# A planner that charges TensorE for entering and leaving narrow tiles, in a two-layer diffusion step on one core

## The chip, the core and the metric

The kernel runs on one of the eight cores of one Trainium2 chip. The metric is the device time of one execution in microseconds (us). The core has four engines that compute: TensorE (PE in the profile; its weight loads are PEld), VectorE (DVE), ScalarE (ACT) and GpSimd (POOL). SyncE (SP) only issues DMAs here. Each engine runs its own list of instructions in order, and waits on semaphores where an operand comes from another engine or from a DMA.

## The reference

Two layers (DEPTH = 2) act on 640 tokens of width 2048, 128 of a prompt and 512 of a sample. Per layer, cut to what matters:

```python
shift, scale, gate = split(silu(c) @ w_ada[l] + b_ada[l], 3)      # adaLN
h = rmsnorm(x, norm_pre[l]) * (1 + scale) + shift
qa, ka, va, za, beta, alpha, cq, ckv, kpe, zb, xc, zc = split_cols(h @ w_in[l])
oa = delta_branch(...)    # 8 heads, gated DeltaNet, forward and backward
ob = mla_attend(...) * silu(zb)          # 4 heads of latent attention
oc = multiscale_pool(...) * silu(zc)     # 4 pooling groups
y = concatenate([oa, ob, oc]) @ w_out[l]
x = x + gate * rmsnorm(y, norm_post[l])

def gated_delta_chunked(...):            # inside delta_branch, per head and direction
    lmat = where(strict, einsum(kb, k) * decay, 0)
    sol = triangular_solve(lmat + eye, [kb * exp(gc), v * beta], lower, unit)
    s, o = scan over the chunks          # state update and output
```

The outputs are the two token streams after both layers, the normalised latents and rotary keys of the prompt, and the final states of its scans. Everything is float32.

## The kernel before

The kernel has no hand-written order. `Body` (line 502 on) calls operations through a recorder (`Sched.record`), in the order of the model: `consts`, `start`, then `phase_a(l)` and `phase_b(l)` for the two layers. `Sched.run` (line 350) then plans: it plays an event-driven model of the engines forward, and whenever an engine is free in that model it takes from the engine's heap the ready operation with the lowest priority number, which is the order of recording unless `later` shifts it. An operation becomes ready when its inputs are done in the model plus a latency from the table `LAT` (line 163: 0.45 us from TensorE to VectorE or ScalarE, 0.5 us back), and its buffers are granted. The length of an operation comes from `cost` (line 209): for TensorE a few hundredths of a us and the columns over 2400 per us, doubled for 3.4 us after an idle time of 3.4 us. The state of the port that VectorE and GpSimd share is the variable `port`. `issue` (line 469) emits the planned order, so all instructions of the trace carry line 499. The priorities, the latencies and the costs therefore decide what stands beside what, and nothing else does; the instructions that exist are the same whatever the costs, apart from operations that may go to one of two engines (`either`, line 309): copies and scalings to ScalarE or VectorE, and in `rest` (line 752) the remainder of a split to GpSimd or VectorE.

Full products are split in two float32r parts, high and low, so each costs three matmuls (`win_group`, line 783, for `w_in`; `product` in `phase_b` for `w_out`). In the trace they read from `slabr`, 128 rows by 256, 384 or 512 columns. These are the bulk of TensorE's work, about 12,000 of its 17,259 products and transposes. They depend on little, and the planner uses them to fill the time while TensorE waits for other things.

Narrow tiles are weights with fewer than 128 rows, or with 32 columns. They occur in three places:

- `ada_rows` (line 1457): the adaLN products, in bursts of 4 in `start` (256 columns wide) and of 16 later (128 wide), with a weight tile of 128x32 (`128*32` in the trace). After a burst `ada_sum` (line 1466) copies the sums out on ScalarE and transposes them.
- `delta` (line 1183), in each of the eight heads. The decay matrix of each of ten blocks of 128 tokens is inverted in steps. The 32x32 diagonal blocks go out to DRAM (`sd`, the name `d` in the trace), come back as 40 rows, and are solved on VectorE in 31 steps of two operations; the result goes to DRAM and comes back. Then TensorE joins the blocks: 20 products of 32x32, a VectorE copy of 128x160 (`T1`), 30 products of 32x32, copies on ScalarE and VectorE (`COPY slab<-psum 32x160` four times), 10 products of 64x64, a ScalarE copy (`T2`), and 10 more of 64x64. Between these bursts the planner puts full products of the next head's `head_in` (line 891), whose convolutions (`conv_tile`, line 841) are VectorE steps of 128x642.
- small transposes in `consts`, `start`, `consts2`, `gates` and `phase_b`.

After the joining, `delta` runs five dependent steps of the recurrence in both directions and ends in four and one transposes of the output.

Of the kernel before, what the change touches and what calls it, by code (L numbers as in the profile page):

```python
# [151 lines left out]
def cols(x):  # L152
    n = 1
    for s in x.shape[1:]:
        n *= s
    return n


class Sched:
# [190 lines left out]
    def run(self):  # L350
        self.prepare()
        ev = []
        seq = 0
        engs = ["PE", "DVE", "ACT", "POOL", "SP"]
        free = {e: True for e in engs}
        heap = {e: [] for e in engs}
        hw = 0.0
        bus = 0.0
        last, warm, port = -10.0, 0.0, 0.0

        def push(o):
            for e in {o.eng, *o.alts}:
                heapq.heappush(heap[self.ENG[e]], (o.pr, o))

        for op in self.ops:
            if op.need == 0:
                push(op)
        now = 0.0
        done = 0
        order = []  # L370
        again = []

        def retry(tags):
            for g in tags:
                for o in g.waiting.pop(g.next, ()):
                    o.parked = False
                    push(o)

        every = [g for g in self.tags.values() if g.space != "D"]
        while True:  # L380
            for e in engs:
                while free[e] and heap[e]:
                    pr, op = heapq.heappop(heap[e])
                    if op.placed or op.parked:
                        continue
                    new = [t for t in op.tiles if t.slot is None]
                    miss = None
                    for t in new:
                        if not self.grant(t):
                            miss = t  # L390
                            break
                        if t.tag.space != "D":
                            again.append(t.tag)
                    if miss is not None:
                        op.parked = True
                        miss.tag.waiting.setdefault(miss.n, []).append(op)
                        continue
                    op.placed = True
                    if self.ENG[op.eng] != e:
                        (op.eng, op.meth, op.a, op.k, op.cost, op.lock), = [(n, *x) for n, x in op.alts.items() if self.ENG[n] == e]  # L400
                    op.start = now
                    op.seq = len(order)
                    order.append(op)
                    if op.meth == "dma_start":
                        hw = max(hw, now) + 0.45
                        op.bus = max(bus, hw)
                        bus = op.bus + op.nbytes / 340e3
                        op.end = max(bus, hw + 0.3) + 2.0
                    else:
                        cost = op.cost  # L410
                        if e == "PE":
                            if now - last > 3.4:
                                warm = now + 3.4
                            if now < warm:
                                cost *= 2
                            last = now + cost
                        op.end = now + cost
                        if op.lock:
                            op.end = max(now, port) + cost
                            port = op.end  # L420
                    free[e] = False
                    heapq.heappush(ev, (now + op.cost if op.meth == "dma_start" else op.end, 0, seq, e))
                    heapq.heappush(ev, (op.end, 1, seq, op))
                    seq += 1
            if again:
                retry(again)
                again = []
                if any(free[e] and heap[e] for e in engs):
                    continue
            if not ev:  # L430
                break
            now = ev[0][0]
            rel = False
            while ev and ev[0][0] <= now + 1e-9:
                _, kind, _, x = heapq.heappop(ev)
                if kind == 0:
                    free[x] = True
                elif kind == 1:
                    done += 1
                    eng = self.ENG[x.eng]  # L440
                    for t in x.tiles:
                        t.left -= 1
                        if t.left == 0 and t.tag.space != "D":
                            heapq.heappush(ev, (now + self.FREE[t.tag.space], 3, seq, t))
                            seq += 1
                    for s in x.succ:
                        s.need -= 1
                        lat = self.LAT["DMA" if x.meth == "dma_start" else eng][self.ENG[s.eng]]
                        s.ready = max(s.ready, now + lat)
                        if s.need == 0:  # L450
                            heapq.heappush(ev, (s.ready, 2, seq, s))
                            seq += 1
                elif kind == 3:
                    g = x.tag
                    g.used[x.slot] = None
                    x.dead = True
                    while g.low < len(g.tiles) and g.tiles[g.low].dead:
                        g.low += 1
                    rel = True
                else:  # L460
                    push(x)
            if rel:
                retry(every)
        if done != len(self.ops):
            waits = [(o.i, o.eng, o.meth, [t.tag.name for t in o.tiles if t.slot is None]) for o in self.ops if not hasattr(o, "end") and o.need == 0]
            raise RuntimeError(f"stuck: {done} of {len(self.ops)}: {waits[:5]}")
        self.order = order
# [1199 lines left out]
```

## Time and profile before

| | before |
|---|---|
| median of 3 runs | 2635.76 us (2635.53 to 2638.45) |
| the profiled execution | 2642.71 us, its span 2640.6 us |
| mean granted clock of TensorE | 0.982 |
| TensorE busy | 2541.0 us (96%) |
| VectorE, ScalarE, GpSimd busy | 1664.4, 1026.8, 739.7 us (63%, 39%, 28%) |
| moved by DMA | 347.98 MB |

Span times run from the first instruction to the last of the profiled execution; the rest of its own time lies around them. A row such as `128*128 128x256` is a weight tile of 128 rows by 128 columns with a moving operand of 128x256; a float32 product is two records, a float32r product or a transpose is one. Starts overlap: a matmul's own duration includes its way through the array, so the pace is read from one start to the next.

### The profile page before, as it was taken

Reading aid. Unit: us, or ns where it says so; the run is one execution under the profiler, and the core shown is the slowest. Engines: PE = TensorE matmul, PEld = TensorE weight load, DVE = VectorE, ACT = ScalarE, POOL = GpSimd, SP = SyncE. Lnnn points to the kernel's source line nnn. Section 1 sums busy time; section 2 is a strip of 40 time slices with the busy share of each in tenths; the row PEclk is TensorE's granted clock in tenths of the full one; section 3 lists DMA queues with packets and bytes.
Section 4 is the critical chain, followed back from the end, with each engine's and each line's share of the span. In section 5 each row is a group of like instructions: output and inputs, shape, how many; then the busy total and the mean of one; then the engine's idle time right before and its main releaser. Section 6 shows DMA issues by size and latency. Waiting matters only on the chain.

```text
span 2640.6 us, 52982 instructions
## 1 busy us (share of the span) xinstructions
PE 2541.0 (96%) x20553; PEld 2380.4 (90%) x20553; DVE 1664.4 (63%) x4229; ACT 1026.8 (39%) x2789; POOL 739.7 (28%) x825
## 2 busy tenths in 40 slices
PE   4999999999999999999988999999999999999998
PEld 1689999999999998878888999999999999988888
DVE  3545556888888886332257365678878887755225
ACT  3233345444444432222247333444444444323222
POOL 0021112354333333220025211233444333334002
PEclk7999999999999999999998999999999999999999
DMA  9944444332343333896755434523433334336225
GB/s 314 335 108 110 133 116 121 96 95 83 92 103 101 102 91 100 235 271 173 190 182 157 126 95 126 149 78 91 101 103 90 91 92 103 84 84 194 92 75 191
DMA packets 541202, 347.98 MB, mean 132 GB/s; under 512 B 103826, under 2 KB 499734, under 8 KB 540310
## 3 DMA queue, kind: packets, MB, share of 16 engines
q1 hardware_dynamic: 540950, 344.59, 46.7%
q8 instruction: 162, 2.65, 0.4%
q14 instruction: 90, 0.74, 0.1%
HBM read 313.07 MB, written 31.46 MB: 130 GB/s over the span
## 4 chain that ended last, share of the span: by engine, by line
PE 80%; DMA 6%; DVE 3%; ACT 2%; POOL 1%; issue 1%; SPq 1%; DVEq 0%; ACTq 0%
PE psum L499 80%; DVE slab L499 3%; DMA slab<-d 2%; DMA slab<-in_w_in_dram 1%; DMA slab<-in_w_ada_dram 1%; ACT slab L499 1%; POOL slabr L499 1%; DMA slabW<-in_w_ada_dram 1%; DMA d<-slab 1%; SPq L499 1%; ACT slabr L499 1%; ACT slabW L499 0%; DMA slab<-in_x_sample_dram 0%; DVE slabV L499 0%; DMA slabW<-d 0%
## 5 line engine op out<-in xcount | busy, mean ns | idle before, releaser
L499 PE MATMUL psum<-slabr 128*128 128x384 f32 (+2 forms) x11760 | 2011.1, 324 | 2.3 <-DVE slabW L499 1.0
L499 PEld LDWEIGHTS psum<-slabr 128*128 128x128 f32 x11760 | 1778.2, 190 | 86.9 <-issue 23.5
L499 POOL TENSOR_TENSOR slabr<-slab,slabr 128x512 fp32r<-128x512 f32 (+3 forms) x428 | 482.8, 1136 | 1200.3 <-ACT slabr L499 878.8
L499 ACT ACTIVATE slabr<-slab 128x512 fp32r<-128x512 f32 (+3 forms) x731 | 393.3, 548 | 879.2 <-PE psum L499 726.5
L499 DVE TENSOR_TENSOR slabr<-slab,slabr 128x512 fp32r<-128x512 f32 (+3 forms) x404 | 262.8, 654 | 416.1 <-ACT slabr L499 363.8
L499 PE MATMUL psum<-slab 128*128 128x128 f32 (+4 forms) x4375 | 434.7, 256 | 56.7 <-DVE slab L499 31.9
L499 DVE TENSOR_TENSOR slab<-slab 128x5 f32<-128x5 f32 (+20 forms) x1298 | 473.2, 376 | 19.2 <-DMA slab<-d 3.9
L499 ACT ACTIVATE slab<-psum 128x128 f32<-128x128 f32 (+6 forms) x823 | 276.1, 351 | 492.5 <-PE psum L499 384.7
L499 PEld LDWEIGHTS psum<-slab 128*128 128x128 f32 (+4 forms) x4375 | 352.1, 140 | 97.5 <-DVE slab L499 39.3
L499 DVE SCALAR_TENSOR_TENSOR slab<-slab 128x5 f32<-128x5 f32 (+7 forms) x618 | 348.2, 572 | 42.9 <-ACT slab L499 33.9
L499 ACT ACTIVATE slab<-slab 128x642 f32<-128x642 f32 (+4 forms) x240 | 141.1, 603 | 62.3 <-DVE slab L499 55.7
L499 DVE COPY slab<-psum 32x160 f32<-32x160 f32 (+9 forms) x214 | 84.0, 399 | 112.7 <-PE psum L499 98.0
L499 DVE TENSOR_SCALAR slab<-slab 128x1 f32<-128x1 f32 (+7 forms) x363 | 111.4, 326 | 29.0 <-ACT slabW L499 16.2
L499 POOL TENSOR_SCALAR slab<-slabV,slab 128x128 f32<-128x128 f32 x128 | 58.1, 460 | 217.5 <-PE psum L499 216.9
L499 DVE SCALAR_TENSOR_TENSOR slab<-psum,slab 128x128 f32<-128x128 f32 (+1 forms) x216 | 80.1, 378 | 56.4 <-PE psum L499 54.5
L499 DVE TENSOR_REDUCE slab<-psum 128x4 f32<-128x16 f32 (+3 forms) x104 | 39.5, 380 | 106.5 <-PE psum L499 105.3
L499 PE MATMUL psum<-slab,slabW 32*32 32x32 f32 (+2 forms) x1216 | 80.8, 219 | 14.5 <-DMA slab<-d 7.8
L499 POOL TENSOR_TENSOR slab<-slab 128x640 f32<-128x640 f32 (+5 forms) x46 | 68.1, 1481 | 95.1 <-ACT slab L499 77.8
L499 ACT ACTIVATE slab<-psum,slab 128x256 f32<-128x256 f32 (+2 forms) x93 | 58.7, 641 | 78.3 <-DVE slab L499 74.6
L499 PEld LDWEIGHTS psum<-slab,slabW 32*32 32x32 f32 (+2 forms) x1216 | 66.3, 132 | 23.1 <-DMA slab<-d 10.7
L499 DVE SCALAR_TENSOR_TENSOR slab<-slab,psum 128x128 f32<-128x128 f32 (+2 forms) x160 | 62.0, 395 | 37.2 <-PE psum L499 25.9
L499 PE MATMUL psum<-slab,slabV 128*128 128x128 f32 (+1 forms) x352 | 72.4, 296 | 1.9 <-DVE slab L499 1.4
(61 smaller groups left out, 1384.5 us busy)
## 6 DMA issues: line engine op xcount, KB each, us to landing
slab<-in_w_in_dram SPq DMA_DIRECT2D x186, 512.0 KB
slab<-in_w_ada_dram SPq DMA_DIRECT2D x32, 1024.0 KB
slabW<-in_w_ada_dram SPq DMA_DIRECT2D x32, 1024.0 KB
slab<-in_w_out_dram SPq DMA_DIRECT2D x64, 512.0 KB
slabW<-d SPq DMA_DIRECT2D x64, 320.0 KB
slabV<-in_w_ada_dram SPq DMA_DIRECT2D x32, 512.0 KB
slabW<-in_w_ada_dram SPq DMA_DIRECT2D x32, 512.0 KB
d<-slab SPq DMA_DIRECT2D x32, 320.0 KB
```

The lines of the kernel that those rows point to most:

```text
L499: op.inst = getattr(getattr(nc, op.eng), op.meth)(*[real(x) for x in op.a], **{n: real(x) for n, x in op.k.items()})
```

## The change

The planner's loop gets one more state, `narrow`: whether TensorE's last placed operation had a narrow weight. Where the next one differs, its cost in the plan grows by 0.1 us on the way in and by 0.27 us on the way out. The instructions are as before but for the engine of those that may go to two.

```diff
@@ -356,7 +356,7 @@
-        last, warm, port = -10.0, 0.0, 0.0
+        last, warm, port, narrow = -10.0, 0.0, 0.0, False
@@ -409,6 +409,10 @@
                         cost = op.cost
                         if e == "PE":
+                            part = op.a[1].shape[0] < 128 or cols(op.a[1]) == 32
+                            if part != narrow:
+                                cost += 0.1 if part else 0.27
+                            narrow = part
                             if now - last > 3.4:
                                 warm = now + 3.4
```

The 17,259 products and transposes of TensorE stay, with 339 changes between narrow and other tiles before and 333 after. VectorE has 47 operations fewer and GpSimd 39 more; ScalarE has 8 more. Lines behind the change are four higher, so line 499 is 503 after.

The first place is VectorE in head 2 of layer 0, from the copy `T1` to the four copies that the 64x64 products need. `128x642` is a convolution step. Before:

```order
L499 COPY slab<-psum 128x160
L499 SCALAR_TENSOR_TENSOR slabV_3862<-psum,slab,slabW_3582 128x128 x2
L499 SCALAR_TENSOR_TENSOR slabW_3582<-psum,slab,slabW_3582 128x128 x2
L499 SCALAR_TENSOR_TENSOR slab<-slab 128x642
L499 STREAM_TRANSPOSE slabV_3862<-slabW_3582 32x160 x4
L499 SCALAR_TENSOR_TENSOR slab<-slab 128x642
L499 COPY slab<-psum 32x5x32 x4
L499 SCALAR_TENSOR_TENSOR slab<-slab 128x642
```

After, on the same stretch:

```order
L503 COPY slab<-psum 128x160
L503 SCALAR_TENSOR_TENSOR slabV_3862<-psum,slab,slabW_3555 128x128 x2
L503 SCALAR_TENSOR_TENSOR slabW_3555<-psum,slab,slabW_3555 128x128 x2
L503 SCALAR_TENSOR_TENSOR slab<-slab 128x642
L503 STREAM_TRANSPOSE slabV_3862<-slabW_3555 32x160 x4
L503 COPY slab<-psum 32x5x32 x4
L503 SCALAR_TENSOR_TENSOR slab<-slab 128x642
```

The convolution step that stood ahead of the four copies now stands behind them.

The second place is TensorE in head 5 of layer 0, from the first 32x32 burst to the first 64x64 burst, with full products (`slabr`) between. Before:

```order
L499 MATMUL psum<-slab,slabW_3582 32x32 x20
L499 MATMUL psum<-slabr 128x256 x3
L499 MATMUL psum<-slabr 128x384 x2
L499 MATMUL psum<-slabr 128x256 x6
L499 MATMUL psum<-slab 32x32 x30
L499 MATMUL psum<-slab 128x128 x4
L499 MATMUL psum<-slabr 128x256 x6
L499 MATMUL psum<-slabr 128x384 x5
L499 MATMUL psum<-slab,slabW_3582 64x64 x10
```

After:

```order
L503 MATMUL psum<-slab,slabW_3555 32x32 x20
L503 MATMUL psum<-slabr 128x256 x3
L503 MATMUL psum<-slabr 128x384 x4
L503 MATMUL psum<-slab 32x32 x30
L503 MATMUL psum<-slab 128x128 x4
L503 MATMUL psum<-slabr 128x384 x8
L503 MATMUL psum<-slab,slabW_3555 64x64 x10
```

Between the first two bursts 11 full products became 7, and between the second and third 11 became 8.

The third place is TensorE at the end of head 6 of layer 0, up to the four transposes of its output (the last row). Before:

```order
L499 MATMUL psum<-slabr 128x384 x2
L499 MATMUL psum<-slab 128x128 x4
L499 MATMUL psum<-slabr 128x384 x6
L499 MATMUL psum<-slabr 128x256 x12
L499 MATMUL psum<-slabr 128x384
L499 MATMUL psum<-slab 128x128
L499 MATMUL psum<-slabr 128x384 x7
L499 MATMUL psum<-slab,slabV_3862 128x128
L499 MATMUL psum<-slabr 128x384 x28
L499 MATMUL psum<-slab,slabV_3862 128x512
L499 MATMUL psum<-slab 128x128 x4
```

After:

```order
L503 MATMUL psum<-slabr 128x256 x2
L503 MATMUL psum<-slab 128x128 x4
L503 MATMUL psum<-slabr 128x256 x9
L503 MATMUL psum<-slabr 128x384 x10
L503 MATMUL psum<-slab 128x128
L503 MATMUL psum<-slabr 128x384 x2
L503 MATMUL psum<-slabr 128x256 x8
L503 MATMUL psum<-slab,slabV_3862 128x128
L503 MATMUL psum<-slabr 128x256 x4
L503 MATMUL psum<-slabr 128x384 x36
L503 MATMUL psum<-slab,slabV_3862 128x512
L503 MATMUL psum<-slab 128x128 x4
```

The full products in this stretch were 56 and are 71.

## Rows read from the trace of the kernel before

**Rows 1.** The page: span, engines (busy us, share, instructions), and chain by engine.
```profile
span 2640.6 us, 52982 instructions
...
PE 2541.0 (96%) x20553; PEld 2380.4 (90%) x20553; DVE 1664.4 (63%) x4229; ACT 1026.8 (39%) x2789; POOL 739.7 (28%) x825
...
PE 80%; DMA 6%; DVE 3%; ACT 2%; POOL 1%; issue 1%; SPq 1%; DVEq 0%; ACTq 0%
```

**Rows 2.** TensorE's waits: total us, times, longest us.
```profile
PE psum L499 <- DVE slab L499: 36.1, 20, 6.7
...
PE psum L499 <- DMA slab<-d: 7.8, 10, 1.4
```

**Rows 3.** Timeline, TensorE, change of layer: start, us, instruction [idle before, releaser].
```profile
1384.36 0.69 PE L499 MATMUL psum<-slab 128*128 128x128 f32 x2 [6.86 <-ACT slab L499]
```

**Rows 4.** Timeline, TensorE, an adaLN burst.
```profile
1058.55 0.60 PE L499 MATMUL psum<-slab 128*128 128x128 f32 x4
1059.08 1.08 PE L499 MATMUL psum<-slabW,slab 128*32 128x128 f32 x32
1060.09 0.71 PE L499 MATMUL psum<-slab,slabV 128*128 128x128 f32 x4
```

**Rows 5.** Timeline, TensorE, joining in head 2 of layer 0.
```profile
671.03 0.73 PE L499 MATMUL psum<-slab,slabW 32*32 32x32 f32 x40
671.69 1.93 PE L499 MATMUL psum<-slabr 128*128 128x256 f32 x14
673.55 2.17 PE L499 MATMUL psum<-slab 32*32 32x32 f32 x64
...
679.29 1.17 PE L499 MATMUL psum<-slab,slabW 64*64 64x64 f32 x20 [1.52 <-ACT slab L499]
```

**Rows 6.** Timeline, TensorE, joining in head 5 of layer 1.
```profile
2201.48 0.73 PE L499 MATMUL psum<-slab,slabW 32*32 32x32 f32 x40 [1.40 <-DMA slab<-d]
...
2204.34 3.52 PE L499 MATMUL psum<-slab 32*32 32x32 f32 x64
```

**Rows 7.** Windows: stretch, us, busy (instructions) of PE, PEld, DVE, ACT, POOL, clock, DMA.
```profile
132.00:138.00 6.00, 6.00 (x53) 4.07 (x51) 3.65 (x9) 1.20 (x2) 1.52 (x2) 1.00 0.13 30
2204.00:2211.00 7.00, 7.00 (x92) 6.46 (x92) 4.61 (x12) 3.20 (x9) 1.28 (x1) 0.59 0.17 26
```

**Rows 8.** Timeline, VectorE, the same stretch of head 2.
```profile
673.05 0.32 DVE L499 COPY slab<-psum 128x160 f32<-128x160 f32 x1
...
676.52 1.43 DVE L499 SCALAR_TENSOR_TENSOR slab<-slab 128x642 f32<-128x642 f32 x1
677.88 1.31 DVE L499 COPY slab<-psum 32x160 f32<-32x160 f32 x4
```

**Rows 9.** Timeline, TensorE, output transposes of head 6, layer 0.
```profile
1034.03 0.70 PE L499 MATMUL psum<-slab 128*128 128x128 f32 x4 [1.61 <-DVE slab L499]
```

**Rows 10.** Timeline, TensorE, adaLN products in `phase_b` of layer 0.
```profile
1094.07 1.08 PE L499 MATMUL psum<-slabW,slab 128*32 128x128 f32 x32 [1.49 <-DMA slabW<-in_w_ada_dram]
1095.08 5.52 PE L499 MATMUL psum<-slabr 128*128 128x384 f32 x34
1102.90 1.08 PE L499 MATMUL psum<-slabW,slab 128*32 128x128 f32 x32 [2.30 <-DMA slabW<-in_w_ada_dram]
```

**Rows 11.** Groups of TensorE by form: busy us, mean ns | idle before, releaser.
```profile
L499 PE MATMUL psum<-slabr 128*128 128x384 f32 x4800 | 1002.7, 344 | 1.0 <-ACT slabr L499 0.9
L499 PE MATMUL psum<-slabr 128*128 128x256 f32 x5520 | 799.5, 288 | 1.0 <-DVE slabW L499 1.0
```

**Rows 12.** Timeline, TensorE, the last adaLN products of the start.
```profile
138.15 0.64 PE L499 MATMUL psum<-slabW,slab 128*32 128x256 f32 x8
```

**Rows 13.** Timeline, VectorE and GpSimd, solve steps and a remainder.
```profile
654.43 0.23 DVE L499 TENSOR_TENSOR slab<-slab 40x87 f32<-40x87 f32 x1
...
654.85 1.08 DVE L499 TENSOR_TENSOR slab<-slab 40x87 f32<-40x87 f32 x1
...
654.54 1.29 POOL L499 TENSOR_TENSOR slabr<-slab,slabr 128x512 fp32r<-128x512 f32 x1 [2.04 <-ACT slabr L499]
```

## The prediction

> **What bounds the kernel.** I read the page's engine table and chain first. TensorE is busy for 2541.0 of 2640.6 us and carries 80% of the chain that ended last [rows 1]. So the time is TensorE's own work plus what it waits for, and an order can change only the second part, about 100 us. The table of waits says who ends them: VectorE in 20 of them (36.1 us) and the DMAs that bring back a head's solved blocks in 10 (7.8 us) [rows 2]. The timeline shows that a large share of the rest is structural: at the change of layer TensorE waits 6.86 us for the normalised rows [rows 3]. The new order has the same products, the same transposes and the same VectorE and ScalarE steps there, so that wait stays.
>
> **What the change does to the order.** No instruction is added or removed; the planner's clock for TensorE alone changes, by 0.1 us on entering and 0.27 us on leaving a narrow tile. It does not make the planner gather narrow tiles: the built orders have 339 changes between narrow and full tiles before and 333 after. What it does change is how much other work the planner believes has passed. The trace gives the true price. Four 128-wide products take 0.53 us up to a burst of 16 narrow ones (32 records), and that burst takes 1.01 us to the next start [rows 4]. The planner had this burst at 16 x (0.01 + 128/2400) = 1.01 us, and now has it at 1.38. So the old plan was right for this burst within the entry, while the new one is 0.37 us too long, or 0.28 us if the entry costs 0.09 us more than it was charged (0.53 against 4 x 0.109, the planner's price for the four transposes). For 20 products of 32x32 the old plan had 20 x 0.0668 = 1.34 us, the new one 1.71, and the trace has 0.66 us to the next start [rows 5]. The new clock overcharges bursts: where an answer is awaited across one, TensorE gets there 0.3 to 0.4 us earlier than planned; where a long chain on VectorE is awaited, the plan puts in other work.
>
> **Terms, on the profiled execution's 2642.7 us (span 2640.6 and 2.1 around it).** It lies 0.26% over the median of the runs, 2635.8; I take the same change off the median.
>
> Solve waits. A head's first 32x32 products wait for blocks that come back by DMA: 1.40 us in head 5 of layer 1 [rows 6], the longest of the ten. Between a head's last key-query product (line 1244) and this read, I counted TensorE's work at the paces of undisturbed neighbours: 72.6, 70.5 and 70.0 us in heads 3, 4 and 5 before, and 74.3, 71.3 and 75.5 us after, while VectorE's work in the same stretch is no longer than it was. The waits there are 0.97, 1.05 and 0.74 us in layer 0 and 0.78, 0.98 and 1.40 in layer 1 (the row, and five like it); the added 1.7, 0.8 and 5.5 us take off 5.5 of their 5.9 us. Bounds: 0 (VectorE late by as much) and 7.8, all such waits [rows 2].
>
> The clock behind a wait. After the 1.40 us wait the granted clock falls to 0.59 in the next stretch, the lower of the two levels (1.2 GHz) for most of it [rows 7]; the 64 small products take 3.52 us there [rows 6] against 2.17 in head 2 of layer 0, where no wait came before them [rows 5]. Their 1.35 us, and as much again for the full tiles about them, are 3 us that go with the wait. Bounds 0 and 3.
>
> VectorE in head 2. TensorE waits 1.52 us at the 64x64 products [rows 5] because VectorE does a 642-wide convolution step of 1.43 us just before the four copies (1.31 us) that these products need [rows 8]. The new order has that step behind the copies. The same happens in layer 1: 2 x 1.52 = -3.0 us. Bounds 0 and -3.0. In head 5 the new order puts such a step in front of other work that the copies follow; I charge the like of one head, 3.0 us over both layers, as the cost of queues that I cannot see. Bounds 0 and 8, twice the longest and a clock fall.
>
> End of the heads. The output of head 6 is awaited 1.61 us [rows 9] (1.27 us in layer 1). From its last product on, 56 fp32r products stood before its four transposes and 71 do now. At 5.52 us for 34 [rows 10] the 15 give 2.4 us, more than either wait: -2.9 us. The two waits for w_ada behind it, 1.49 and 2.30 us [rows 10], have 21 and 38 products before them in place of 14 and 34: 11 x 0.162 = -1.8 us. Bounds for both: 0 and -6.7.
>
> Prologue. Here the change costs. The planner's clock loses more to the many bursts of four, and 43 fewer full products stand before the last transposes of the start (144 stand behind them, 101 before); at 0.145 us, the busy time per 128x256 product [rows 11], that is 6.2 us of work put off. TensorE cannot win it all back by being early, since it waits for w_ada there. But the DMA engines are only 0.13 busy from 132 us on, so the last w_ada tile is there by then, and TensorE reads it at 138.15 [rows 7, 12]: it is 5 us behind its loads. So 5 of the 6.2 us are only moved, and +1.2 is lost. Bounds 0 and 6.2.
>
> Short trips. This is the term against the change. In each head's solve three answers are fetched across narrow bursts. Counted at 0.145 and 0.209 us (the busy time of a 128x384 product [rows 11]), the filler between the first two bursts falls from a mean of 1.73 to 1.31 us over the 16 heads, between the second and third from 2.31 to 1.99, and between the third and fourth from 1.76 to 1.30: 1.2 us a head, 19 us in all. In head 2 the copy ends at 673.37 us and TensorE reads it at 673.55 [rows 5, 8], so there is next to no spare there, and yet no wait is seen; the copy was late because VectorE was busy with a convolution step until it began at 673.05, while TensorE had sent its burst at 671.03 to 671.76. Elsewhere the answer takes 0.6 us less. I take a third, +6 us, because VectorE's waits are only 20 in the whole run. Bounds 0 and 19.
>
> Six fewer changes at 0.09 us: -0.5. The sum is -5.5 - 3.0 - 3.0 + 3.0 - 2.9 - 1.8 + 1.2 + 6.0 - 0.5 = -6.5 us: 2636.2 for the profile, 2629 for the median, 0.25% less. What a measurement of this kernel can tell from no change is about 0.2%, or 5.3 us.
>
> **A rule weighed.** The trace shows a change of tile size costing about 0.09 us on the way in [rows 4]. The Trainium skill, "TensorEngine Tiling (Array Packing)", section Key Properties, says that changing the tiling mode drains TensorE; it has no time for it. Were the drain as long as the planner's 0.37 us a pair, the new plan would be the true one, the short trips would lose nothing, and the sum by that reading would be -12.5 us; by the row it is -6.5.
>
> **Rivals.**
> No change that can be measured: the waits that go are given back elsewhere in the delta heads, half of the short trips' 19 us in place of a third and the prologue's 6.2 us in full; -6.5 + 3.5 + 5.0 = +2, about 2637. For it speaks that TensorE is full and the products are the same; against it that head 2 and the solve waits are placed differently in both layers.
> Slower, by short trips: TensorE comes to the three reads of each solve, and to the transposes behind each burst of adaLN products, before VectorE or ScalarE has answered. If two thirds of the 19 us become waits and four of these reach 1.4 us and pull the clock down at 3 us each, the sum is -6.5 + 6.5 + 12 = +12, 2648. It decides from the point where more than half of the trips have under 0.4 us to spare; the read at 673.55 speaks for it, the 20 waits against it.
> Slower, by the port: the new order has 39 more operations on GpSimd and 47 fewer on VectorE. A VectorE solve step of 0.23 us took 1.08 us while a GpSimd remainder of 1.29 us ran [rows 13], ending with it. If every added remainder held up a solve step by 0.85 us, the solves would grow by 39 x 0.85 = 33 us, 2 us in each head, less the 0.4 us that each remainder leaves on VectorE, 16 us: the solve waits come back and the sum is -6.5 + 8.5 + 6 = +8, 2644. The Trainium skill, "SBUF — State Buffer", section SBUF: two separate sides, says that the port pair that both share is locked for a whole instruction and the loser blocks; the trace agrees, at 1.08 against 0.23 us. Against it: the planner already holds the one engine for the other, and in heads 3 to 5 the VectorE work of the solve gets less.
>
> **Numbers.** Forecast (faster, -6 to -20) 0.44; no measurable change 0.34; slower by short trips 0.16; slower by the port 0.06. So faster 0.44, same 0.34, slower 0.22. The gains' far bounds are -7.8 - 3 - 3 - 6.7 = -20 with no cost, 2615; the cost side reaches 2648. The range is 2614 to 2648; the forecast's own is 2615 to 2630.
>
> **What would show it.** Right: waits for the solve's DMA under 3 us in all; no wait of 1.5 us at the 64x64 products of head 2; none over 0.5 us before head 6's transposes; the last start transposes near 142 us. Wrong: more than 30 waits for VectorE, or new stretches at the lower clock between 430 and 1030 us; the prologue ending with TensorE idle for more than 5 us beyond what it is; a solve step count as before with longer steps.

## The result and the profile after

The change makes the kernel slower: 2673.99 us median (2672.61 to 2674.70, 4 runs) against 2635.65 (2635.51 to 2638.45, 4 runs). The ratio is 1.0142, 95% interval 1.0125 to 1.016. The forecast was 2629 with a range to 2648, so the sign is wrong and the range misses the time by 26 us.

The profiled execution took 2672.61 us. Its page answers to [rows 1]:

```profile
span 2670.8 us, 52968 instructions
...
PE 2555.4 (96%) x20553; PEld 2389.0 (89%) x20553; DVE 1675.6 (63%) x4182; ACT 1024.9 (38%) x2797; POOL 788.5 (30%) x864
...
PE 79%; DMA 12%; DVE 5%; ACT 2%; SPq 1%; issue 1%; POOL 0%; DVEq 0%; ACTq 0%; POOLq 0%
```

The span is 30.2 us longer. TensorE does the same 20,553 records, yet is busy 14.4 us longer, so about half of the loss is hidden in "busy". In the chain the share of DMAs went from 6 to 12%. The table of TensorE's waits (total, times, longest) has more and other waits than [rows 2]:

```profile
PE psum L503 <- DVE slab L503: 33.8, 24, 6.0
PE psum L503 <- ACT slab L503: 14.4, 9, 6.8
PE psum L503 <- DMA slab<-d: 14.2, 12, 2.5
PE psum L503 <- DMA slabW<-in_w_ada_dram: 9.7, 16, 3.5
```

The waits for solved blocks rose from 7.8 to 14.2 us. Those for w_ada (this row and two smaller ones) rose from 13.6 to 17.5 us. Summed over the whole view, TensorE waits 100.2 us in place of 86.3.

Where it lies: I took the start of the same product in both traces at the borders of the stages. The heads of layer 0 (from the first transposes of head 0 to the last product of the first column group of `phase_b`) take 784.1 us in place of 765.2, those of layer 1 747.8 in place of 740.1, the start 1.5 us more, and the rest within 3 us. So 26.6 of the 30 us are in the heads. I split them by the pace of like pairs of neighbouring products at the full clock: 13.6 us are added waits, and 12.8 us are added time in stretches of low clock (26.1 us against 13.3). Everything else cancels. The trace's own records say nearly the same: in the heads the waits are 41.1 us against 27.9, and the granted clock is at its lower level for 51.2 us against 27.4, of which half is lost.

The stretches follow waits. This is TensorE in head 2 of layer 0, to be read against [rows 5]:

```profile
675.28 1.62 PE L503 MATMUL psum<-slabr 128*128 128x256 f32 x9
678.42 0.73 PE L503 MATMUL psum<-slab,slabW 32*32 32x32 f32 x40 [1.52 <-DMA slab<-d]
679.08 2.77 PE L503 MATMUL psum<-slabr 128*128 128x256 f32 x11
681.78 3.52 PE L503 MATMUL psum<-slab 32*32 32x32 f32 x64
684.95 2.59 PE L503 MATMUL psum<-slabr 128*128 128x256 f32 x10
687.47 2.03 PE L503 MATMUL psum<-slab,slabW 64*64 64x64 f32 x20
```

The 1.52 us wait that stood at the 64x64 products is gone, as forecast; but as much stands at the first 32x32 products now, where none was before, and the 64 records behind it (30 small products and four transposes) take 3.52 us instead of 2.17. The windows (stretch, us, five engines' busy time and instructions, granted clock, DMA share, GB/s) show the clock behind this wait, behind the wait for blocks in head 7, and behind a wait for w_ada:

```profile
679.00:694.00 15.00, 15.00 (x144) 13.71 (x138) 7.36 (x18) 4.63 (x12) 0.92 (x2) 0.54 0.38 102
1065.00:1076.00 11.00, 10.06 (x134) 9.17 (x135) 3.43 (x11) 1.22 (x3) 0.00 (x0) 0.53 0.21 54
1120.00:1127.00 7.00, 5.96 (x49) 5.61 (x50) 0.00 (x0) 0.00 (x0) 2.99 (x3) 0.51 1.06 267
```

That is the lower of the two levels (1.2 GHz) for nearly all of 15, 11 and 7 us. The waits ahead of the last two, on TensorE's timeline:

```profile
1065.93 1.10 PE L503 MATMUL psum<-slab,slabW 32*32 32x32 f32 x40 [2.54 <-DMA slab<-d]
...
1121.04 1.93 PE L503 MATMUL psum<-slabW,slab 128*32 128x128 f32 x32 [3.47 <-DMA slabW<-in_w_ada_dram]
```

The second answers to [rows 10], where the two waits were 1.49 and 2.30 us.

Why do the solved blocks come later? From the end of a head's solve on VectorE to the first 32x32 product it takes 11.5 us in the mean over the 16 heads, against 9.7 before. SyncE's queue shows one reason in head 7 of layer 0. Before:

```profile
1032.45 0.33 SPq L499 DMA_DIRECT2D slabV<-in_w_pool_dram  x1
1035.21 3.50 SPq L499 DMA_DIRECT2D d<-slab  x6
1039.07 4.74 SPq L499 DMA_DIRECT2D slab<-d  x9
```

After:

```profile
1052.30 0.33 SPq L503 DMA_DIRECT2D slabV<-in_w_pool_dram  x1
1052.72 2.11 SPq L503 DMA_DIRECT2D d<-slab  x5
1054.93 0.57 SPq L503 DMA_DIRECT2D slab<-in_w_in_dram  x1
1055.61 3.78 SPq L503 DMA_DIRECT2D slab<-d  x6
1059.50 0.99 SPq L503 DMA_DIRECT2D slab<-in_w_in_dram  x1
1061.65 2.32 SPq L503 DMA_DIRECT2D slab<-d  x3
```

The nine loads of the blocks went out in one piece before; now a w_in load stands among them and the last three leave 1061.65 to 1063.97 us, which is when the 2.54 us wait is made. The stores are late too: five of them leave from 1052.72 on, behind a w_pool load and behind the end of the solve at 1052.37, where all six left from 1035.21 on before, with the solve ending at 1037.60. In head 4 two w_in loads stand ahead of the stores:

```profile
823.30 7.76 SPq L503 DMA_DIRECT2D slab<-in_w_in_dram  x2
831.15 1.67 SPq L503 DMA_DIRECT2D d<-slab  x4
835.47 0.80 SPq L503 DMA_DIRECT2D slab<-d  x2
```

The second of them waits for its buffer until a GpSimd remainder is done. SyncE's waits in the stretch from 822 to 841 us say so:

```profile
SPq L503 <- POOL slabr L503: 9.1, 2, 6.9
```

The solve ended at 829.66 us and its first stores left at 831.15; before, the first left 1.75 us ahead of the end of the solve. Over the 16 heads, the last of the nine loads leaves SyncE 9.2 us after the end of the solve in the mean, against 7.4 before. That is the whole of the 1.8 us by which the mean trip grew.

### The profile page after: what moved, and what is told of

It reads as the page before. It is cut to its first block, busy times and chain, and to the rows that moved or that the text cites. A ratio compares the mean times of both kernels' runs of the same rounds, so it can differ in the third digit from the quotient of the medians.

```text
span 2670.8 us, 52968 instructions
## 1 busy us (share of the span) xinstructions
PE 2555.4 (96%) x20553; PEld 2389.0 (89%) x20553; DVE 1675.6 (63%) x4182; ACT 1024.9 (38%) x2797; POOL 788.5 (30%) x864
## 3 DMA queue, kind: packets, MB, share of 16 engines
q1 hardware_dynamic: 540950, 344.59, 46.1%
## 4 chain that ended last, share of the span: by engine, by line
PE 79%; DMA 12%; DVE 5%; ACT 2%; SPq 1%; issue 1%; POOL 0%; DVEq 0%; ACTq 0%; POOLq 0%
PE psum L503 79%; DVE slab L503 4%; DMA slabW<-in_w_ada_dram 3%; DMA slab<-d 2%; DMA slab<-in_w_in_dram 1%; SPq L503 1%; DMA slab<-in_w_ada_dram 1%; ACT slab L503 1%; DMA d<-slab 1%; DMA d<-slabV 1%; DMA slabW<-d 1%; DMA slabV<-in_w_ada_dram 1%; DMA slab<-in_x_prompt_dram 0%; POOL slabr L503 0%; DMA slab<-in_x_sample_dram 0%
## 5 line engine op out<-in xcount | busy, mean ns | idle before, releaser
L503 POOL TENSOR_TENSOR slabr<-slab,slabr 128x512 fp32r<-128x512 f32 (+2 forms) x469 | 532.5, 1145 | 1186.3 <-ACT slabr L503 898.7
L503 DVE TENSOR_TENSOR slabr<-slab,slabr 128x512 fp32r<-128x512 f32 (+3 forms) x363 | 250.3, 694 | 416.1 <-ACT slabr L503 386.3
L503 PE MATMUL psum<-slab 128*128 128x128 f32 (+4 forms) x4375 | 441.3, 257 | 61.9 <-DVE slab L503 30.5
L503 DVE TENSOR_TENSOR slab<-slab 40x240 f32<-40x240 f32 (+21 forms) x1298 | 482.1, 383 | 27.2 <-DMA slab<-d 11.5
L503 ACT ACTIVATE slab<-psum 128x128 f32<-128x128 f32 (+7 forms) x817 | 273.1, 350 | 511.1 <-PE psum L503 407.3
L503 DVE SCALAR_TENSOR_TENSOR slab<-slab 128x5 f32<-128x5 f32 (+7 forms) x618 | 350.7, 576 | 57.7 <-ACT slab L503 53.1
L503 DVE COPY slab<-psum 32x160 f32<-32x160 f32 (+7 forms) x220 | 88.1, 407 | 111.1 <-PE psum L503 99.1
L503 DVE TENSOR_SCALAR slab<-slab 128x1 f32<-128x1 f32 (+9 forms) x367 | 124.3, 358 | 23.1 <-ACT slabW L503 11.5
L503 POOL TENSOR_SCALAR slab<-slabV,slab 128x128 f32<-128x128 f32 x128 | 65.4, 519 | 241.4 <-PE psum L503 240.9
L503 PE MATMUL psum<-slab,slabW 32*32 32x32 f32 (+2 forms) x1216 | 82.5, 223 | 19.9 <-DMA slab<-d 14.2
L503 PEld LDWEIGHTS psum<-slab,slabW 32*32 32x32 f32 (+2 forms) x1216 | 68.3, 136 | 28.2 <-DMA slab<-d 17.4
```

What stands on the lines that cost most here:

```text
L503: op.inst = getattr(getattr(nc, op.eng), op.meth)(*[real(x) for x in op.a], **{n: real(x) for n, x in op.k.items()})
```

## The experiments

Each edit is against the changed kernel, unless it says otherwise. Ratios are to the kernel before, on the same chip. The first four ask which part of the charge costs, and whether its size matters.

**A tenth of the charge.**
```diff
-cost += 0.1 if part else 0.27
+cost += 0.01 if part else 0.027
```


> The charge is cut to a tenth: 0.01 us on the way in, 0.027 us on the way out. The plan's order still differs from that before from TensorE's operation 237 on. Theory A (size): the loss of 38 us comes from the planner's TensorE clock being 0.37 us too long for each burst, so a tenth of it costs a tenth at most: 2636 to 2640 us. Theory B (reshuffle): any small change of the clock reorders the eight delta heads of both layers, and which order comes out is luck; then this lies anywhere between about 2620 and 2675, and a value more than 6 us away from before with a charge this small speaks for B.

Measured: 2642.22 us, 1.0012 (0.9998 to 1.0026). That is 4 us over the kernel before on the same chip (2638.26), under the 6 us that were to speak for B, and 2 us over A's range. Size, then, by the bound set; but within it the waits for blocks are 13.3 us, nearly those of after.

**Only the narrow tiles of the heads.**
```diff
-part = op.a[1].shape[0] < 128 or cols(op.a[1]) == 32
+part = op.a[1].shape[0] < 128
```


> The full charge (0.1 and 0.27 us), but only for weights with fewer than 128 rows: the bursts of the delta heads and a few small transposes; the 32-column adaLN products are planned as before. In the trace of after the added time lies in the heads (20 us in layer 0, 10 in layer 1). Theory A (size, in the heads): as after, 2665 to 2680. Theory B (reshuffle): another order of the heads, so anywhere between 2620 and 2675.

Measured: 2662.38, 1.0087 (1.0066 to 1.0108): a little under what A said, and within B's wide bounds.

**Only the adaLN products.**
```diff
+part = op.a[1].shape[0] == 128 and cols(op.a[1]) == 32
```


> The full charge, but only for the 32-column adaLN products (128 rows); the bursts of the heads are planned as before. Theory A: the heads are not charged, so no more than the adaLN part of the loss is seen, 2633 to 2641. Theory B: the charge in the start alone shifts what is left over when the heads begin, so their order changes and the time can move by 6 us or more either way.

Measured: 2650.07, 1.0040 (1.0027 to 1.0053), over A's 2641, so B's reading fits better here. Yet the waits differ by place. Those for w_ada are 12.5 us with the charge in the heads alone and 16.2 with it on the adaLN products alone (13.6 before). Those inside the recurrence of the heads are 8.9 us in the first and 3.6 in the second (3.1 before, 7.7 after). For the recurrence this alone shows nothing of the charge: the plan without any charge and with the engine choice of before, further below, has 7.7 us there too.

**The charge, with the engine choice of the plan before.** Each operation that may go to one of two engines is fixed ahead of planning, from a list.
```diff
+for op, b in zip([o for o in self.ops if o.alts], side, strict=True):
+    if b == "1":
+        (op.eng, op.meth, op.a, op.k, op.cost, op.lock), = [(n, *x) for n, x in op.alts.items()]
+    op.alts = {}
```


> The full charge as in after, but each operation that may go to one of two engines goes where the plan before the change put it (245 operations differ between the two plans). Theory C (engine choice): the longer solves of heads 2, 3 and 5 (59.4, 59.5 and 60.9 us against 55.0, 56.8 and 55.7) come from VectorE steps held up by added GpSimd remainders, so at least half of the 38 us goes: 2655 or less, with solves within 1 us of before. Theory A: as after, 2665 to 2680. Theory B: anywhere between 2620 and 2675, with solves no shorter as a rule.

Measured: 2649.33, 1.0037 (1.0024 to 1.0050): most of the loss is gone, as C said. But not for C's reason: the solves of heads 2, 3 and 5 are 60.3, 49.5 and 56.9 us, one longer than in after and two shorter. It is the waits for blocks that went, to 5.9 us, and no low clock is left in the heads. The waits for w_ada are 23.0 us, more than in after, and those inside the recurrence 9.2.

The next two move only SyncE's queue; the order on the four computing engines is kept.

**w_in loads behind the solve's DMAs, on the plan of after and on that of before.**
```diff
+for sd in [t for t in self.tags["D"].tiles if t.shape == [3, 10, 128, 32]]:
+    trip = [o for o in order if sd in o.tiles][2:]
+    sp = [o for o in order if o.eng == "sync"]
+    i, j = sp.index(trip[0]), sp.index(trip[-1])
+    for w in sp[max(0, i - 3):j]:
+        if w.tiles[0].tag.name == "raw" and w not in trip:
+            ...   # move w behind trip[-1], but ahead of its first user
```


> The plan of after, with the instructions of TensorE, VectorE, ScalarE and GpSimd in exactly the order of after. Only SyncE's queue is changed: in each head the w_in loads that stand between or just ahead of the stores and loads of the solved blocks (34 loads over both layers) are moved behind them, as far as their first user allows. Theory Q (queue): in after a w_in load that waits for a GpSimd remainder stands ahead of the stores, so in head 4 they go out 1.5 us after the solve's end where they went out 1.75 us before it, and the blocks are read 10.2 to 13.6 us after the solve's end against 8.3 to 10.9 before; the queue then gives back most of the 6.3 us of added waits for solved blocks and the clock falls behind them: waits for blocks from 14.2 us to under 7, and 2650 to 2664. Theory S (solve length): the solves of heads 2, 3 and 5 are longer and that is what TensorE waits for; the return trip is a minor part: 2666 to 2676.

> The same move of w_in loads (36) in SyncE's queue, on the plan of before. The waits for solved blocks are 7.9 us there. Theory Q: they fall under 4 us and the clock falls with them in layer 1: 2628 to 2634. The rival is that w_in loads come later and TensorE waits for them instead: 2640 or more.

Measured: 2720.22, 1.0310 (1.0294 to 1.0325), and 2699.02, 1.0228 (1.0212 to 1.0243). Both misses in time, but the edit did to the queue what it should: the last load of the blocks leaves 7.6 and 6.9 us after the end of the solve in the mean (9.2 in after, 7.4 before), and the waits for blocks are gone entirely, none is in the view. In their place the full products wait for weights that came late. Those of 128x256 waited 0.1 us in after and 1.0 before [rows 11]; now, in the first and the second of the two:

```profile
L513 PE MATMUL psum<-slabr 128*128 128x256 f32 x5520 | 808.8, 291 | 36.2 <-POOL slabr L513 19.6 <-ACT slab L513 8.7 <-DVE slabW L513 7.9
L509 PE MATMUL psum<-slabr 128*128 128x256 f32 x5520 | 812.2, 291 | 35.8 <-ACT slab L509 24.9 <-DVE slabW L509 5.6 <-POOL slabr L509 5.1
```

Behind these waits the clock was low as well, for 118 and 114 us past the first 70 us of the span (82 in after, 58 before). So SyncE's queue decides who waits, the burst or the full products, and it has no slack for a few us of w_in either.

**The charge doubled, and on one side only.**
```diff
-cost += 0.1 if part else 0.27
+cost += 0.2 if part else 0.54     # doubled
+cost += 0.1 if part else 0.0      # entering only
```


> The charge doubled: 0.2 us in, 0.54 us out. Theory A (size): the loss grows with the charge, so more than after: 2690 to 2720. Theory B (reshuffle): the size doesn't matter once the order is another one: 2640 to 2680, as likely below after as above it.

> The charge on entering only, 0.1 us, near the 0.09 us that the trace of before shows for the adaLN burst; nothing on leaving. Theory A: the planner's clock is then as true as before or truer, so the time is that of before within 0.3%: 2630 to 2646. Theory B: anywhere between 2620 and 2675.

Measured: 2682.30, 1.0164 (1.0145 to 1.0183), and 2631.18, 0.9976 (0.9967 to 0.9985). Doubling the charge adds little to the time, less than A said and 2 us more than B did. It does double the waits for w_ada, to 34.2 us, and the 64x64 products now wait 13.2 us where they waited 3.8 before. The groups by form (busy, mean ns | idle before) show the latter, doubled charge first in

```profile
L503 PE MATMUL psum<-slab,slabW 64*64 64x64 f32 x320 | 19.6, 228 | 13.2 <-issue 13.2
```

and entering only in

```profile
L503 PE MATMUL psum<-slab,slabW 64*64 64x64 f32 x320 | 18.9, 222 | 2.9 <-ACT slabr L503 2.3 <-issue 0.6
```

Entering only lies within A's bounds, and beats both kernels, the one before by 0.24%. Its waits for w_ada are 9.0 us, those for blocks 17.4, more than in after:

```profile
PE psum L503 <- DVE slab L503: 25.7, 19, 5.9
PE psum L503 <- DMA slab<-d: 17.4, 14, 2.6
```

**Leaving only, half of both, and two neighbours of entering only.**
```diff
+cost += 0.0 if part else 0.27     # leaving only
+cost += 0.05 if part else 0.135   # half
+cost += 0.08 if part else 0.0     # and 0.12
```


> Nothing on entering, the full 0.27 us on leaving. In the trace of before a burst of 16 adaLN products takes to the next start just what the old plan gave it, so this part of the charge has no counterpart on the chip. Theory A (the part that is too long makes the loss): as after or near it, 2655 to 2680, with more and longer waits for VectorE, ScalarE and w_ada behind bursts. Theory B (reshuffle): a value anywhere between 2620 and 2675; under 2645 would speak for it.

> Half of both charges (0.05 and 0.135 us). Theory A: between before and after, 2642 to 2664. Theory B: not bound to lie between them.

> Entering alone at 0.08 us, a neighbour of the 0.1 that gave 0.24% off. Were that gain the reward of a truer price, the neighbour has it too: 2627 to 2634. Were it the luck of one order, the neighbour scatters about before: 2630 to 2650.

> Entering alone at 0.12 us, the neighbour on the other side. By the truer price 2627 to 2636, by luck 2630 to 2650.

Measured: 2665.04, 1.0092 (1.0077 to 1.0108); 2659.92, 1.0078 (1.0060 to 1.0095); 2637.15, 0.9995 (0.9985 to 1.0004); 2645.79, 1.0028 (1.0018 to 1.0037). The charge on leaving costs, at half its size too. The gain of entering only is not a truer price: 0.02 us to either side it is gone. Orders that differ by so little scatter by 0.5%, from 0.9976 to 1.0028.

**No charge, with the engine choice fixed as in after, or as in before** (the list of above, on the kernel before).

> No charge; each operation that may go to one of two engines goes where the plan of after put it. Theory C (engine choice): the return trips of the solved blocks stay long (mean over 11 us, 9.7 before) and the time stays above before by 0.5% or more: 2652 to 2670. Theory A (charge alone): the waits at bursts are back at those of before (15 us with the adaLN products) and the time is that of before within the scatter of orders that the small charges showed, 0.3%: 2630 to 2646.

> No charge and the engine choice of before, fixed ahead of planning, as the control for the run with the full charge and the same choice (2649, 0.37% above before). Theory A: the charge alone is worth the difference between the two, and this one comes out at 2632 to 2642. If fixing the choice by itself moves the time, it comes out elsewhere, and the run with the charge can't be read as the charge alone.

Measured: 2648.00, 1.0033 (1.0022 to 1.0045), and 2641.14, 1.0012 (1.0001 to 1.0022). The first is over A's range and under C's, the second is in A's. With a fixed choice the charge costs 0.25% (1.0037 against 1.0012) and the new choice 0.2%. Together they cost 1.4%. The two don't add up to it: 1.0% belongs to the plan that has both. The trips of the blocks take 11.0 us with the new choice alone and 10.8 with the old one; so the new choice doesn't lengthen them more than the old one, though both are over the 9.7 us of before.

**The changed kernel once more.**

> The changed kernel once more, for its profile. If the low clock in its heads follows from where its waits stand, the stretches come again behind the waits for solved blocks of head 2 and head 7 and the w_ada wait of layer 0, some 50 us of low clock after 400 us as before; if it is a matter of chance they stand elsewhere. Time 2672 to 2676 either way.

Measured: 2677.69, 1.0148 (1.0126 to 1.0169). Head 2 waits as long as in the first profile, and its clock stays up; head 5's falls instead, which was at 1.00 in the first profile behind a wait of 2.17 us. The windows, head 5's of the first profile in the first line, then the two of this second profile:

```profile
922.00:937.00 15.00, 11.78 (x189) 10.55 (x188) 11.25 (x26) 6.86 (x17) 1.26 (x3) 1.00 0.47 105
679.00:694.00 15.00, 14.15 (x204) 13.12 (x205) 10.59 (x28) 8.05 (x24) 1.94 (x4) 1.00 0.41 102
921.50:936.50 15.00, 14.70 (x163) 13.27 (x165) 8.54 (x19) 4.28 (x12) 0.87 (x2) 0.54 0.37 101
```

and TensorE's timeline of the second, with the waits ahead of both:

```profile
679.45 0.73 PE L503 MATMUL psum<-slab,slabW 32*32 32x32 f32 x40 [1.51 <-DMA slab<-d]
680.11 1.84 PE L503 MATMUL psum<-slabr 128*128 128x256 f32 x11
681.88 2.17 PE L503 MATMUL psum<-slab 32*32 32x32 f32 x64
...
685.44 1.17 PE L503 MATMUL psum<-slab,slabW 64*64 64x64 f32 x20
...
921.80 0.73 PE L503 MATMUL psum<-slab,slabW 32*32 32x32 f32 x40 [1.99 <-DMA slab<-d]
922.46 2.29 PE L503 MATMUL psum<-slabr 128*128 128x256 f32 x7
924.68 3.52 PE L503 MATMUL psum<-slab 32*32 32x32 f32 x64
```

So the order does not fix which wait pulls the clock down; it changed from one execution to the next. The sum changed less: 23.4 us in the heads this time, 26.1 the first, 13.3 before.

All orders with a free engine choice, by the profiled execution of each (low clock: time at the lower level past the first 70 us of the span):

| charge in / out, us | waits of TensorE, us | of these for w_ada | for blocks | low clock, us | time, us |
|---|---|---|---|---|---|
| 0.1 / 0 | 82.4 | 9.0 | 17.4 | 46.1 | 2632.5 |
| 0.08 / 0 | 84.0 | 10.5 | 10.8 | 46.2 | 2636.2 |
| before | 86.3 | 13.6 | 7.8 | 57.7 | 2642.7 |
| 0.12 / 0 | 86.4 | 14.3 | 8.8 | 43.2 | 2642.5 |
| 0.01 / 0.027 | 88.8 | 12.5 | 13.3 | 52.7 | 2645.2 |
| adaLN only | 92.5 | 16.2 | 12.1 | 55.3 | 2651.3 |
| 0 / 0.27 | 98.9 | 18.4 | 14.8 | 62.7 | 2660.4 |
| heads only | 99.8 | 12.5 | 16.6 | 69.8 | 2662.6 |
| after, 0.1 / 0.27 | 100.2 | 17.5 | 14.2 | 81.7 | 2672.6 |
| 0.05 / 0.135 | 101.0 | 17.6 | 8.2 | 59.2 | 2661.6 |
| 0.2 / 0.54 | 124.5 | 34.2 | 7.8 | 56.5 | 2684.4 |

The time follows the sum of the waits and the low clock, and not any one kind of wait. Taking the waits and half of the time at the lower clock off the time leaves 2527 to 2535 us in every row, though the times differ by 52 us; the six profiles that are not in the table leave 2524 to 2533. So TensorE's own work is the same, and after differs from before by 13.9 us of waits, 12.0 of clock and 4 that this sum doesn't place. The waits alone don't do: after, half of the charge and heads only have nearly the same waits, and after is 10 to 11 us longer, 6 to 11 of them by its clock. With a charge of 0.135 us or more on leaving the adaLN products, the waits for w_ada are 16 us or more in every order; without, at most 14.3. The waits for blocks scatter between 7.8 and 17.4 us without regard to the charge.

## Why the prediction was wrong, step by step

**What bounds the kernel: right.** TensorE is 96% busy in both.

**The true price of the change of tiles: wrong in part.** The prediction timed a burst up to the next start, 1.01 us, and called the old plan right for it and the new one 0.37 or 0.28 us too long. The trace of before has a cost on the way out as well, which shows in the starts at the full clock, away from waits. A full product of 128x256 takes 0.120 us to the next full one in the median, 0.209 where a narrow one follows, and 0.223 where a narrow one went before it; with 384 columns the three are 0.174, 0.268 and 0.279. The next but one is back at the usual pace. So in [rows 5] the 14 full products between two bursts take 1.86 us, and not 14 x 0.120 = 1.68. The last product of a burst takes a further 0.1 us longer than those within it: after the change, two bursts stand in a row and take 1.90 us, not 2 x 1.01:

```profile
1110.10 1.97 PE L503 MATMUL psum<-slabW,slab 128*32 128x128 f32 x64
1112.00 0.66 PE L503 MATMUL psum<-slab 128*128 128x128 f32 x4
```

So entering costs about 0.09 us and leaving about 0.2. A burst of 16 with both is 1.01 + 0.09 + 0.10 = 1.20 us; the plan before had it at 1.01, the plan after at 1.38, and the one with half of the charge at 1.20. For 20 products of 32x32, 0.66 + 0.19 us, the plan before was too long already at 1.34, and the charge adds to that. (The four records of [rows 4] are two float32 products and no transposes; the starts give the 0.09 us all the same. By the planner's own condition there are 338 changes before and 334 after, not 339 and 333; that hardly moves the -0.5.)

That a charge on leaving costs time held: with nothing on leaving the time stays within 0.3% of before; with half of it or more on all narrow tiles, and a free engine choice, it is 0.8 to 1.6% longer. That it costs because it is longer than the truth is not shown: half of the charge has the adaLN burst right, and still loses 0.8% and waits 17.6 us for w_ada.

**Solve waits, -5.5 us: the step that failed, by 11.9 us with the sign turned** (7.8 to 14.2, +6.4). I counted that TensorE has 0.8 to 5.5 us more work ahead of the read and held the other side fixed. It did not hold. From the last key-query product to the read, head 5 of layer 0 went from 75.6 to 82.9 us: the solve from 55.7 to 60.9, with 73 other operations of VectorE in it (33.1 us) in place of 69 (29.1 us), and the trip from 9.2 to 11.8. Over the whole stretch VectorE did 105 such operations in place of 107, much as the prediction had counted; more of them stood within the solve. In heads 6 and 7 the trips grew by 2.1 and 5.3 us, by what stands in SyncE's queue. I had looked at VectorE's work in these heads, but not at SyncE's queue, and the bound of 0 that I gave for "VectorE late by as much" left out that it may be late by more.

**The clock, -3.0: failed, by 16 us.** It went +12.8. I took one low stretch as gone with its wait; new waits of 1.5 to 3.5 us brought several, as rival 2 had it, though priced at 12 us on top of 6.5.

**VectorE in head 2, -3.0, and unseen queues, +3.0: right in both.** The wait of 1.52 us at the 64x64 products of head 2 is gone in both layers (also in the second profile, where the clock was full there), and others have come at these products in heads 0, 4 and 5 (all of them 3.8 us before, 4.0 after).

**End of head 6, -2.9: failed.** 15 more products stand before the transposes, and they wait still:

```profile
1044.49 0.66 PE L503 MATMUL psum<-slab 128*128 128x128 f32 x4 [1.37 <-DVE slab L503]
```

1.61 us became 1.37 in layer 0 [rows 9], and 1.27 became 1.37 in layer 1: the output comes later by about as much as the 15 products take. This is the same fault: cover counted on one engine alone.

**w_ada, -1.8: failed.** The two waits that it meant went from 3.79 us to 3.47, and all waits for w_ada from 13.6 to 17.5. The counts of products ahead of the bursts were right. The second wait is gone, but the first grew from 1.49 to 3.47 us: its load left SyncE 1.2 us after the burst ahead of it began, and 1.0 us before that burst in the old order. The other added waits for w_ada stand where the term had none.

**Prologue, +1.2: right.** The start is 1.5 us longer. The last adaLN products of the start, at 138.15 before [rows 12], are read at

```profile
134.83 0.64 PE L503 MATMUL psum<-slabW,slab 128*32 128x256 f32 x8
```

and the start's last transposes end 3.2 us earlier; the full products come later by as much and a little more.

**Short trips, +6.0: right in size by luck.** The waits inside the joining and the recurrence are 12.6 us against 6.9. But of the added 5.7 us only 1.1 stand in the joining, where the term put all of them; 4.6 stand in the recurrence, which has no narrow tiles and which it did not name. One third of the lost cover did not become waits at the three reads.

**The rule weighed: nearer than it was taken to be.** The Trainium skill ("TensorEngine Tiling (Array Packing)", Key Properties) says that changing the tiling mode drains TensorE. The trace agrees that a change costs: 0.09 us on the way in and about 0.2 on the way out, 0.3 a pair, where the planner charged 0.37 and the prediction saw 0.09. Yet the sum that went with the rule, -12.5, was further off than -6.5: a truer price did not bring a shorter time. By the time alone entering cannot be judged, since 0.08, 0.1 and 0.12 us scatter by 0.5%.

**The rivals.** The nearest was the second, slower by short trips: right in sign and in kind (waits, and the clock behind them), short by 26 us, because it left the solve's trips at their old length. The port is not it: the 16 solves take 846.1 us in sum against 844.6, and their steps themselves 413 us against 421.

**What stays open.** At half its size or more on all narrow tiles, the charge on leaving costs 0.8% and more wherever the engine choice is free, and on the adaLN products it raises the waits for w_ada; that is shown, and so is that waits and the low clock behind them make up the time. Why such a charge brings waits, though it is near the true price, is not settled. Nor is why the plan of after loses 1.4%, where charge and choice alone lose 0.2% each: its long trips are seen and come from SyncE's queue, but moving the w_in loads that lengthen them costs more than it gives. A plan with the trips shortened in another way, or with the narrow products themselves priced as the trace has them, was not tried.

## What to carry to other kernels

A planner's cost that is nearer the truth for one operation need not give a better plan: with 0.2 us measured on the way out, half of the charge lost 0.8% and no charge on leaving lost nothing. A change of one price moves every queue, and the waits come where two of them no longer meet. So when an order changes, count both sides of each wait, the work ahead of it and the chain that answers, with its DMA queue; more cover on one engine is no gain by itself. And before a small charge is believed or refused, run its neighbours: here 0.08, 0.10 and 0.12 us gave 0.9995, 0.9976 and 1.0028, so one order's gain of 0.2% says nothing of the price. And when a price is read from a trace, look past the next start: half of the cost of leaving a narrow tile stood on the product behind it.

## What was not expected of the hardware

The same program with a wait of 1.5 us at the same place showed the low clock behind it for most of 15 us (0.54) in one execution and the full clock (1.00) in the next, while another wait of the same kind did the reverse; the sum over the heads was alike. A full product behind a narrow burst took 0.1 us longer to the next one (0.223 in place of 0.120 us for 256 columns), on top of the 0.1 us that the burst's own last product took. And a queue of loads with gaps of several us had no slack: 36 of the w_in loads moved by at most 16 places in SyncE's queue cost 2.3%.
